# Ten weight-sum steps moved beside attention, two gate tiles made during the loading of attention's result, and one operand sum moved from GpSimd to VectorE

## The chip, the cores and the metric

The kernel runs on one core of a Trainium2 chip. The core has a matrix engine (TensorE, PE in the profile), a vector engine (VectorE, DVE), an activation engine (ScalarE, ACT), a general engine (GpSimd, POOL) and an engine that mostly issues transfers (SyncE, SP). Each engine works through its own instruction queue in order; semaphores tie the queues together. GpSimd issues transfers too, from the same queue as its arithmetic. The metric is the device time of one execution in microseconds (us), lower is better.

## What is computed

One layer of a streaming encoder on 1024 prompt rows and 32 sample rows, 1056 in all, with D = 1024:

```python
h = rms_norm(x, g_mix)
z = h @ w_in
q, k, v, ch, cb, cc, ga, gb = jnp.split(z, SPLITS, axis=-1)
a = attn_core(q, k, v) @ w_attn_out
u = cc * ch
up = jnp.concatenate([conv_left, u], axis=1)
conv = up[:, 0:n] * conv_w[0]
for j in range(1, CONV_WIDTH):
    conv = conv + up[:, j:j + n] * conv_w[j]
bo = (cb * conv) @ w_conv_out
x = x + (jax.nn.sigmoid(ga) * a + jax.nn.sigmoid(gb) * bo) @ w_mix_out
...
x = x + co @ w_co
hm = rms_norm(x, g_mlp)
x = x + jnp.square(jax.nn.relu(hm @ w_up)) @ w_down
```

The attention is a sliding window of 64-frame chunks with 16 query heads and 4 key heads; between the two parts shown stands a cross-attention into 256 memory tokens.

## The kernel before

Activations lie with features on the 128 partitions. The 1056 rows are three chunks, c = 0, 1, 2, of 384, 384 and 288 columns; D is eight feature tiles, f = 0..7. Every fp32 product is made from two rounded halves of each operand, so a weight tile of 128 x 1024 passes through `issue_w`: a load into `wr` (two buffers), a cast into `wh` on ScalarE (L125) and a subtraction into `wl` on VectorE (L126), three buffers each. A product of one weight tile with one chunk (`gemm`, L183 to L185) is 24 matmuls. Weights are fetched in the order in which items are put on a plan (`item`, `worder`), three ahead.

**Weight sums.** Two products later in the kernel, the gate pairs and the down projection, combine blocks of the weights in a scheme that saves multiplications, and need sums of blocks. GpSimd makes these sums early, one piece at a time, in `sum_step` (L691 to L713): a step starts the load of the next piece (L700 or L702) and then does the four additions (L707) and the store (L711 or L713) of the piece before. Its instructions are pinned to their place in program order. There are 46 pieces, 14 for the gates (`gsum_d`) and 32 for down (`wsum_d`), in two buffers that alternate: `xacc`, and `ws` from the pool `W`. A step's load waits until the store from the same buffer, two pieces earlier, has finished. Where no piece is left, a step does nothing.

**Attention.** 32 hosts, i = 0..31, are items that each carry one attention unit inside a projection: scores before the first chunk, `turn` (transposes) after chunk 1, `values` after chunk 2. A host is a convolution tile (C, H or B), a query tile, a key tile, or, the last one, the gate tile f = 0 (`do_gate`). In C hosts GpSimd multiplies by R (L612), in B hosts too (L627); GpSimd also writes the sink column of each unit's scores (L549). A sum step stands after chunk 1 of hosts 3, 5, ..., 31: 15 steps. The results go to `ao_d` in memory, the last two from GpSimd's queue (L594).

**Behind attention.** `load_attended` (L758 to L763) reads `ao_d` back: per chunk eight tiles, each loaded into a `ct` buffer (six of them), cast on ScalarE and subtracted on VectorE. Around these loads stand a second gate tile (w_in 42) and the eight tiles of attn_out. Attn_out's tile f = 0 is multiplied by the gate that the last host made (`sa`) and stored to `m1_d`; the others are stored unmultiplied to `a_d` by a ScalarE copy (L800). After the items of attn_out stand 24 sum steps and, beside them, `gx_steps`, which make operand combinations for the gate pairs, one of them on GpSimd (n4, L839). Then the seven gate pairs, f = 1..7 (`gate_pair`), each with two weight tiles of w_in and two of sums, make both gates of a tile for chunks 0 and 1 by the scheme and for chunk 2 directly (`gate_c2`); they load attn_out's tile back from `a_d`, multiply and store to `m1_d`. They hold three sum steps each.

**Then** `after_gates` closes the pools of X and of the sums (`W`) and opens `mpool` in their place, for the merged tiles M. `do_conv_out` makes for each chunk and f a product, multiplies it by the gate (L1014), adds the stored attention part (L1015, on GpSimd except for f = 7) and splits the result into M; `do_mix` follows. Accumulators in PSUM are three.

Of the kernel before, what the change touches and what calls it, by code (L numbers as in the profile page):

```python
# [10 lines left out]
F32 = mybir.dt.float32  # L11
F32R = mybir.dt.float32r
AF = mybir.ActivationFunctionType
ALU = mybir.AluOpType
# [4 lines left out]
P = 128  # L19
# [3 lines left out]
CH = [(0, 384), (384, 384), (768, 288)]  # L23
# [15 lines left out]
def hybrid_step(ctx: ExitStack, tc: tile.TileContext, io):  # L39
    nc = tc.nc  # L40
    act, dve, pool_e, pe, sp = nc.scalar, nc.vector, nc.gpsimd, nc.tensor, nc.sync
# [3 lines left out]
    def nm(s):  # L45
        uid[0] += 1
        return f"{s}_{uid[0]}"

    def opened(name, **kw):
        cm = tc.tile_pool(name=name, **kw)  # L50
        return cm, cm.__enter__()
# [10 lines left out]
    ps_cm, ps = opened("ps", bufs=1, space=PSUM)  # L62
# [30 lines left out]
    def pin(ins):  # L93
        return tc.keep_in_program_order(ins)

    def acc_tile(shape):
        return ps.tile(shape, F32, tag="acc", bufs=n_acc, name=nm("acc"))
# [3 lines left out]
    def tmp(n, dt=F32):  # L101
        return tp.tile([P, n], dt, tag="ct", bufs=NCT, name=nm("ct"))

    def slot(pool, tag, n, dt=F32R, bufs=None):
        return pool.tile([P, n], dt, tag=tag, bufs=bufs, name=nm(tag))
# [8 lines left out]
    def item(fn, *keys):  # L114
        plan.append((fn, keys))
        worder.extend(keys)
# [61 lines left out]
    def gemm(out, w, acts):  # L178

        wh, wl = w  # L180
        for k, (hi, lo) in enumerate(acts):
            a = slice(k * P, k * P + P)
            pe.matmul(out, wh[:, a], hi, start=(k == 0), stop=False)  # L183
            pe.matmul(out, wh[:, a], lo, start=False, stop=False)  # L184
            pe.matmul(out, wl[:, a], hi, start=False, stop=(k == len(acts) - 1))  # L185
# [13 lines left out]
    R, RC = [None] * 3, [None] * 3  # L199
# [75 lines left out]
    xg = [[None] * NF for _ in CH]  # L275
# [175 lines left out]
    def after(extras, c):  # L451
        for at, e in extras:
            if at == c:
                e()
# [186 lines left out]
    G = {}  # L641

    def gate_slot(c, f):
        n = CH[c][1]
        return slot(ga_pool, f"Ga{c}", n, F32) if f < 3 else slot(G["pool"], f"Gb{c}", n, F32)
# [1 line left out]
    sg = [[None] * NF for _ in CH]  # L647


    sa = [None] * 3  # L650

    def do_gate(to, extras=()):
        def fn(w):
            for c, (o, n) in enumerate(CH):
                a = acc_tile([P, n])
                gemm(a, w, xg[c])
                t = gate_slot(c, 0)
                dve.tensor_mul(t, a, R[c])
                act.activation(t, t, AF.Sigmoid)
                to(c, t)  # L660
                after(extras, c)

        return fn
# [59 lines left out]
    for i, h in enumerate(hosts):  # L723
        kv, p = i // 8, i % 8
        units = [Unit(kv, p)] + ([Unit(kv, 8)] if p == 7 else [])
        pre = []
        if p == 0:
            pre.append(lambda kv=kv: do_KS(kv))
        pre.append(units[0].scores)
        extras = [(1, units[0].turn), (2, units[0].values)]  # L730
        if i == 0:
            extras = [(0, pre.pop()), (2, units[0].turn)]
            first = units[0].values
        if i == 1:
            extras.insert(0, (0, first))
        if p == 7:
            extras += [(0, units[1].scores), (2, units[1].turn), (2, units[1].values)]
        if i % 2 and i > 1:
            extras.append((1, sum_step))
        if h[0] == "Q":  # L740
            fn, key = do_Q(h[1], h[2], extras), qt(h[1], h[2])
        elif h[0] == "K":
            fn, key = do_K(h[1], extras), ("w_in", 8 + h[1])
        elif h[0] == "G":
            fn, key = do_gate(sa.__setitem__, extras), ("w_in", 34)
        else:
            fn, key = do_conv(*h, extras), conv_w(h[1], h[0])
        item(lambda w, fn=fn, pre=pre: ([e() for e in pre], fn(w)), key)
# [41 lines left out]
    def do_attn_out(f, extras=()):  # L790
        def fn(w):
            for c, (o, n) in enumerate(CH):
                a = acc_tile([P, n])
                gemm(a, w, aop[c])
                t = tmp(n)
                if f == 0:
                    dve.tensor_mul(t, a, sa[c])
                    sp.dma_start(m1_d[c][:, f], t)
                else:
                    act.copy(t, a)  # L800
                    sp.dma_start(a_d[c][:, f], t)
                after(extras, c)

        return fn
# [5 lines left out]
    gop, xq = {}, {}  # L810
# [12 lines left out]
    def gx_split(kind, k, c):  # L823
        hi, lo = gop[kind, k] = (slot(xpool, f"X{c}", 384), slot(xpool, f"X{c}", 384))
        pin(act.copy(hi, xq[kind]))
        pin(dve.tensor_sub(lo, xq[kind], hi.bitcast(F32)))
# [9 lines left out]
        gx_split("b21", k, 0)  # L836

    def gx_rest(k):
        pool_e.tensor_tensor(xq["n4"], xq["b21"], xq["t2"], op=ALU.subtract)  # L839
        sp.dma_start(xs_d["n4"][:, k], xq["n4"])  # L840
        gx_split("t2", k, 1)
        gx_split("n1", k, 1)
# [22 lines left out]
    def close_gates():  # L865
# [6 lines left out]
            wanted.extend((bcp[c], k, bc_d[c][:, k], CH[c][1], lambda c=c: yslot(c)) for k in range(NF))  # L872
        pump(2)

    def gate_pair(f):
        def take(key):
            k, w = ready.pop(0)
            assert k == key, (k, key)  # L880
            return w

        def gate_c2(w):
            n = CH[2][1]
            a = ps.tile([P, n], F32, tag="pt", bufs=2, name=nm("pa"))
            gemm(a, w, xg[2])
            return a

        def into(t, x):
            act.activation(t, x, AF.Sigmoid)  # L890
            return t

        def attended(c, t):
            dve.tensor_mul(t, t, la[c])
            sp.dma_start(m1_d[c][:, f], t)

        la = {}

        def load_a(c):
            la[c] = tmp(CH[c][1])  # L900
            sp.dma_start(la[c], a_d[c][:, f])

        op = lambda kind: [gop[kind, k] for k in range(4)]
        w1 = take(("w_in", 34 + f))
        load_a(0)
        load_a(2)
        A, B, C = (acc_tile([P, 384]) for _ in range(3))
        product(A, w1, 0, op("b11"), True)
        s1 = Y["top"].tile([P, 384], F32, tag="s1", name=nm("s1"))
        act.copy(s1, A)  # L910
        issue_w()
        fetch_w()
        product(A, w1, 1, op("b21"), False)
        attended(0, into(tmp(384), A))
        pump(4 if f == 1 else 1)
        a2 = gate_c2(w1)
        t = tmp(CH[2][1])
        dve.tensor_mul(t, a2, R[2])
        attended(2, into(t, t))
        issue_w()  # L920
        fetch_w()
        w4 = take(("g_sum", f - 1, 0))
        product(B, w4, 0, op("t2"), True)
        load_a(1)
        u2 = Y["top"].tile([P, 384], F32, tag="u2", name=nm("u2"))
        dve.tensor_sub(u2, B, s1)
        sum_step()
        pump(4 if f == 1 else 1)
        w3 = take(("g_sum", f - 1, 1))
        product(C, w3, 1, op("n1"), True)  # L930
        v = Y["top"].tile([P, 384], F32, tag="v", name=nm("v"))
        dve.tensor_add(v, C, s1)
        product(B, w3, 0, op("n3"), False)
        g22 = gate_slot(1, f)
        dve.tensor_sub(g22, B, v)
        sg[1][f] = into(g22, g22)
        pump(0)
        sum_step()
        product(C, w4, 1, op("b22"), False)
        t = tmp(384)  # L940
        dve.tensor_sub(t, C, u2)
        attended(1, into(t, t))
        issue_w()
        fetch_w()
        w2 = take(("w_in", 42 + f))
        product(B, w2, 1, op("n4"), False)
        g21 = gate_slot(0, f)
        dve.tensor_sub(g21, B, s1)
        sg[0][f] = into(g21, g21)
        sum_step()  # L950
        issue_w()
        fetch_w()
        a2 = gate_c2(w2)
        g2 = gate_slot(2, f)
        dve.tensor_mul(g2, a2, R[2])
        sg[2][f] = into(g2, g2)
# [4 lines left out]
    item(lambda: [e() for e in ao(0, range(NF))])  # L961
    b0 = [(0, e) for e in ao(1, range(4))] + [(1, e) for e in ao(1, range(4, NF))] + [(2, e) for e in ao(2, range(4))]
    item(do_gate(hold, b0 + [(2, sum_step)]), ("w_in", 42))
    for f in range(NF):
        extras = [(c, sum_step) for c in range(3)]
        if f == 0:
            extras += [(0, e) for e in ao(2, range(4, NF))]
        else:
            extras += [(c, gx_steps.pop(0)) for c in range(3) if gx_steps]
        item(do_attn_out(f, extras), ("w_attn_out", f))  # L970
# [336 lines left out]
    b11, b21, b22 = (lambda k: xm[0][k]), (lambda k: xm[0][k + 4]), (lambda k: xm[1][k + 4])  # L1307
# [517 lines left out]
```

## Time and profile before

| | |
|---|---|
| median of three runs | 1856.05 us |
| lowest and highest | 1848.42 and 1859.84 us |
| time of the profiled execution | 1858.32 us |
| its span, first to last instruction | 1856.5 us |
| mean granted clock of TensorE | 0.978 |
| bytes moved, mean rate over the span | 330.81 MB, 178 GB/s |

The span is 1.8 us shorter than the profiled execution's own time. Times of single instructions, waits and stages come from that one execution. In rows of the timeline the first number is the start after the span's beginning and the second the duration, in us; brackets give the idle time of the engine just before, and what ended it. "x3" counts instructions. Matmul durations overlap, so that work on TensorE is better read from starts, or from the weight loads (PEld).

### The profile page before, as it was taken

Reading aid. Unit: us, or ns where it says so; the run is one execution under the profiler, and the core shown is the slowest. Engines: PE = TensorE matmul, PEld = TensorE weight load, DVE = VectorE, ACT = ScalarE, POOL = GpSimd, SP = SyncE. Lnnn points to the kernel's source line nnn. Section 1 sums busy time; section 2 is a strip of 40 time slices with the busy share of each in tenths; the row PEclk is TensorE's granted clock in tenths of the full one; section 3 lists DMA queues with packets and bytes.
Section 4 is the critical chain, followed back from the end, with each engine's and each line's share of the span. In section 5 each row is a group of like instructions: output and inputs, shape, how many; then the busy total and the mean of one; then the engine's idle time right before and its main releaser. Section 6 shows DMA issues by size and latency. Waiting matters only on the chain. (4 is left out here: it accounts for less than half of the span.)

```text
span 1856.5 us, 30253 instructions
## 1 busy us (share of the span) xinstructions
PE 1759.0 (95%) x11110; PEld 1737.1 (94%) x11110; DVE 1164.0 (63%) x2158; ACT 795.7 (43%) x1566; POOL 600.5 (32%) x685
## 2 busy tenths in 40 slices
PE   8999999999998999962999989999999989999998
PEld 8999999999998999962999989999999979999997
DVE  6776767667656555533657677776665676435673
ACT  8644535344353333312555655642222333324453
POOL 0013242523424545454224242276555400100001
PEclk9999999999999999985999989999999999999999
DMA  4322232323338888756765657663434488446673
GB/s 174 116 90 97 87 126 81 114 77 111 106 119 283 280 280 276 267 212 206 251 225 182 230 198 256 233 224 119 137 132 141 129 260 261 149 135 196 202 232 130
DMA packets 184291, 330.81 MB, mean 178 GB/s; under 512 B 18817, under 2 KB 140193, under 8 KB 184017
## 3 DMA queue, kind: packets, MB, share of 16 engines
q1 hardware_dynamic: 170368, 280.49, 45.9%
q0 software_dynamic: 13776, 48.41, 7.3%
q8 instruction: 87, 1.43, 0.3%
q14 instruction: 60, 0.48, 0.1%
HBM read 241.86 MB, written 86.97 MB: 177 GB/s over the span
## 5 line engine op out<-in xcount | busy, mean ns | idle before, releaser
L126 DVE TENSOR_TENSOR wl<-wr,wh 128x1024 fp32r<-128x1024 f32 x222 | 294.7, 1328 | 203.7 <-ACT wh L125 203.0
L125 ACT CAST wh<-wr 128x1024 fp32r<-128x1024 f32 x222 | 233.0, 1050 | 440.4 <-PE acc L184 103.6
L183 PE MATMUL acc<-X,wh 128*128 128x384 f32 (+1 forms) x864 | 282.3, 327 | 8.3 <-ACT wh L125 8.3
L184 PE MATMUL acc<-X,wh 128*128 128x384 f32 (+1 forms) x864 | 279.6, 324 | 0.0
L185 PE MATMUL acc<-X,wl 128*128 128x384 f32 (+1 forms) x864 | 278.9, 323 | 0.2 <-DVE wl L126 0.2
L183 PE MATMUL acc<-Y,wh 128*128 128x384 f32 (+1 forms) x624 | 203.5, 327 | 56.6 <-DVE ct L1014 51.9
L184 PE MATMUL acc<-Y,wh 128*128 128x384 f32 (+1 forms) x624 | 203.1, 326 | 1.2 <-DVE Y L763 1.0
L185 PE MATMUL acc<-Y,wl 128*128 128x384 f32 (+1 forms) x624 | 202.8, 325 | 0.0
L259 POOL TENSOR_TENSOR xacc<-xacc,ct 128x384 f32<-128x384 f32 (+1 forms) x62 | 75.6, 1221 | 343.8 <-ACT ct L257 342.0
L183 PEld LDWEIGHTS acc<-Y,wh 128*128 128x128 f32 x624 | 117.8, 189 | 59.3 <-ACT Y L781 52.2
L183 PEld LDWEIGHTS acc<-X,wh 128*128 128x128 f32 x864 | 163.2, 189 | 8.9 <-ACT wh L125 8.3
L184 PEld LDWEIGHTS acc<-X,wh 128*128 128x128 f32 x864 | 163.5, 189 | 0.6
L185 PEld LDWEIGHTS acc<-X,wl 128*128 128x128 f32 x864 | 163.2, 189 | 0.8 <-DVE wl L126 0.8
L184 PEld LDWEIGHTS acc<-Y,wh 128*128 128x128 f32 x624 | 118.0, 189 | 2.7 <-DVE Y L763 2.5
L185 PEld LDWEIGHTS acc<-Y,wl 128*128 128x128 f32 x624 | 118.1, 189 | 0.0
L1571 PE MATMUL acc<-Y,wh 128*128 128x384 f32 (+1 forms) x352 | 113.2, 322 | 0.9 <-DVE lt L1362 0.7
L1572 PE MATMUL acc<-Y,wh 128*128 128x384 f32 (+1 forms) x352 | 113.2, 322 | 0.0
L1573 PE MATMUL acc<-Y,wl 128*128 128x384 f32 (+1 forms) x352 | 112.9, 321 | 0.0
L125 ACT CAST PTh<-pt 128x512 fp32r<-128x512 f32 (+3 forms) x94 | 46.2, 516 | 119.3 <-PE pt L572 111.1
L707 POOL TENSOR_TENSOR xacc<-xacc 128x256 f32<-128x256 f32 x92 | 85.6, 930 | 5.4
L851 PE MATMUL acc<-Y,wh 128*128 128x384 f32 x248 | 83.5, 337 | 2.4 <-DVE ct L1224 1.4
L707 POOL TENSOR_TENSOR ws<-ws 128x256 f32<-128x256 f32 x92 | 82.4, 896 | 5.7
(357 smaller groups left out, 4726.0 us busy)
## 6 DMA issues: line engine op xcount, KB each, us to landing
wr<-in_w_in SPq DMA_DIRECT2D x50, 512.0 KB, 3.5
wr<-in_w_up SPq DMA_DIRECT2D x48, 512.0 KB, 3.8
wr<-in_w_down SPq DMA_DIRECT2D x32, 512.0 KB, 3.8
wr<-wsum_d SPq DMA_DIRECT2D x32, 512.0 KB, 3.7
wl<-wl_d SPq DMA_DIRECT2D x28, 512.0 KB, 4.6
wr<-in_w_conv_out SPq DMA_DIRECT2D x24, 512.0 KB, 4.7
wr<-in_w_mix SPq DMA_DIRECT2D x24, 512.0 KB, 5.1
ct<-b_d SPq DMA_DIRECT2D x48, 192.0 KB, 3.8
```

The lines of the kernel that those rows point to most:

```text
L125: act.copy(hi, src)
L126: dve.tensor_sub(lo, src, hi.bitcast(F32))
L183: pe.matmul(out, wh[:, a], hi, start=(k == 0), stop=False)
L184: pe.matmul(out, wh[:, a], lo, start=False, stop=False)
L185: pe.matmul(out, wl[:, a], hi, start=False, stop=(k == len(acts) - 1))
L259: pool_e.tensor_tensor(acc, acc, sq, op=ALU.add)
L707: pin(pool_e.tensor_tensor(t[:, to], t[:, x], t[:, y], op=ALU.add))
L851: pe.matmul(acc, wh[:, a], hi, start=(start and k == 0), stop=False, skip_group_check=True)
L1571: pe.matmul(a, wh[:, s], hi, start=(start and k == 0), stop=False, skip_group_check=True)
L1572: pe.matmul(a, wh[:, s], lo, start=False, stop=False, skip_group_check=True)
L1573: pe.matmul(a, wl[:, s], hi, start=False, stop=(stop and k == len(acts) - 1), skip_group_check=True)
```

## The change

It has three parts.

1. Hosts 12 to 31 all carry a sum step after chunk 1, where before only the odd ones did. That makes 25 steps in attention instead of 15. The steps behind are left as they were; since the pieces are the same 46, the later ones find none left.
2. Chunk 2 of the first gate, for tiles f = 2 and 3, is made by two new items directly behind the second gate tile, while `ao_d` is read back (`gate_a2`). Their weight tiles, w_in 36 and 37, are fetched for it and fetched again for the gate pairs. The two gates stay in `Gb2` buffers until attn_out's tiles 2 and 3 multiply by them on VectorE (instead of the ScalarE copy) and store to `m1_d`; gate pairs 2 and 3 then neither load chunk 2 of `a_d` nor make that gate.
3. The operand n4 is subtracted on VectorE, pinned, instead of on GpSimd (four times).

`sa` becomes a dictionary with the key (chunk, tile), and `gate_c2` moves out of `gate_pair`.

```diff
-        if i % 2 and i > 1:
+        if i % 2 and i > 1 or i > 11:
             extras.append((1, sum_step))
...
-                if f == 0:
-                    dve.tensor_mul(t, a, sa[c])
+                if (c, f) in sa:
+                    dve.tensor_mul(t, a, sa[c, f])
                     sp.dma_start(m1_d[c][:, f], t)
                 else:
                     act.copy(t, a)
...
     def gx_rest(k):
-        pool_e.tensor_tensor(xq["n4"], xq["b21"], xq["t2"], op=ALU.subtract)
+        pin(dve.tensor_sub(xq["n4"], xq["b21"], xq["t2"]))
...
+    def gate_c2(w):
+        n = CH[2][1]
+        a = ps.tile([P, n], F32, tag="pt", bufs=2, name=nm("pa"))
+        gemm(a, w, xg[2])
+        return a
+
+    def gate_a2(f):
+        def fn(w):
+            a = gate_c2(w)
+            t = sa[2, f] = slot(G["pool"], "Gb2", CH[2][1], F32)
+            dve.tensor_mul(t, a, R[2])
+            act.activation(t, t, AF.Sigmoid)
+
+        return fn
...
         def load_a(c):
+            if (c, f) in sa:
+                return
             la[c] = tmp(CH[c][1])
             sp.dma_start(la[c], a_d[c][:, f])
...
-        a2 = gate_c2(w1)
-        t = tmp(CH[2][1])
-        dve.tensor_mul(t, a2, R[2])
-        attended(2, into(t, t))
+        if (2, f) not in sa:
+            a2 = gate_c2(w1)
+            t = tmp(CH[2][1])
+            dve.tensor_mul(t, a2, R[2])
+            attended(2, into(t, t))
...
     item(do_gate(hold, b0 + [(2, sum_step)]), ("w_in", 42))
+    for f in (2, 3):
+        item(gate_a2(f), ("w_in", 34 + f))
     for f in range(NF):
```

More of the change, by code (lines that the diff above doesn't have):

```diff
@@ L647, in hybrid_step @@
     sg = [[None] * NF for _ in CH]
-    sa = [None] * 3
+    sa = {}
     def do_gate(to, extras=()):
@@ L744, in hybrid_step @@
         elif h[0] == "G":
-            fn, key = do_gate(sa.__setitem__, extras), ("w_in", 34)
+            fn, key = do_gate(lambda c, t: sa.__setitem__((c, 0), t), extras), ("w_in", 34)
         else:
@@ L881, in take @@
             return w
[L883 to L887, printed above, removed]
         def into(t, x):
```

## The prediction

> **What bounds the kernel now.** I read the page's first two parts, then busy time by stage, then the timeline of the one stage where TensorE stops.
>
> ```profile
> span 1856.5 us, 30253 instructions
> PE 1759.0 (95%) x11110; PEld 1737.1 (94%) x11110; DVE 1164.0 (63%) x2158; ACT 795.7 (43%) x1566; POOL 600.5 (32%) x685
> ...
> PE   8999999999998999962999989999999989999998
> ...
> POOL 0013242523424545454224242276555400100001
> PEclk9999999999999999985999989999999999999999
> ```
>
> TensorE is the bound: 95% of the span, full in almost every slice of 46.4 us. The one deep hole is at slices 18 and 19 (6 and 2), and there the granted clock falls too (8 and 5). GpSimd is busy in just those slices. So a saving anywhere else must shorten TensorE's own work, and a saving in the hole can be large. The stages around it (columns: length, busy time and count of each engine, granted clock, DMA share, GB/s):
>
> ```profile
> core 0: us, PE busy (x) PEld busy (x) DVE busy (x) ACT busy (x) POOL busy (x), PEclk, DMA share, GB/s
> ...
> 86.00:556.00 470.00, 470.00 (x3043) 463.36 (x3042) 323.84 (x825) 208.71 (x503) 157.89 (x244) 1.00 0.31 103
> 556.00:582.00 26.00, 20.77 (x111) 17.66 (x110) 16.94 (x27) 10.94 (x23) 13.14 (x19) 1.00 0.84 278
> 582.00:803.60 221.60, 221.60 (x1391) 221.60 (x1390) 125.75 (x168) 79.26 (x140) 107.16 (x130) 1.00 0.82 274
> 803.60:820.40 16.80, 16.80 (x98) 16.68 (x96) 7.07 (x7) 3.88 (x5) 7.91 (x9) 1.00 0.72 252
> 820.40:872.40 52.00, 0.20 (x2) 0.00 (x0) 7.12 (x10) 5.25 (x10) 25.42 (x36) 0.53 0.56 194
> 872.40:940.00 67.60, 66.28 (x364) 65.36 (x365) 44.14 (x66) 32.72 (x56) 17.57 (x15) 0.96 0.70 234
> ```
>
> In order these are attention (32 hosts, 14.7 us each), attention's result loading under attn_out's first tile, attn_out and the gate pairs, the first four conv_out tiles, a stop of 52.0 us, and the rest of conv_out and mix for chunk 0. What ends the stop, in the timeline:
>
> ```profile
> 820.26 0.34 PE L185 MATMUL acc<-Y,wl 128*128 128x384 f32 x1
> ...
> 858.82 0.55 POOL L702 DMA_DIRECT2D ws<-in_w_down  x1 [4.40 <-DMA wsum_d<-ws]
> ...
> 867.20 0.57 POOL L713 DMA_DIRECT2D wsum_d<-ws  x1 [0.41 <-POOL ws L707]
> 870.29 0.51 ACT L125 CAST M<-ct 128x384 fp32r<-128x384 f32 x1 [6.64 <-DMA wsum_d<-ws]
> ...
> 871.78 0.55 DVE L1014 TENSOR_TENSOR ct<-acc,Ga 128x384 f32<-128x384 f32 x1
> ...
> 872.48 0.66 PE L183 MATMUL acc<-Y,wh 128*128 128x384 f32 x1 [51.88 <-DVE ct L1014]
> ```
>
> Read from the bottom up: TensorE waits for a free accumulator, that is for VectorE's eviction L1014; it stands behind the split of the first merged tile M; M waits for the store of the last weight sum. M's pool lies where the sums' buffer `ws` was (`after_gates`). GpSimd still makes weight sums 47 us after TensorE stopped. The stop is a late finish of the sums and nothing else that I can see.
>
> **Part 1, ten more sum steps in attention.** How late are the sums? Each is a load, four additions and a store on GpSimd's queue:
>
> ```profile
> 552.30 0.68 POOL L702 DMA_DIRECT2D ws<-in_w_down  x1
> ...
> 758.72 0.54 POOL L702 DMA_DIRECT2D ws<-in_w_down  x1 [4.64 <-DMA wsum_d<-ws]
> ```
>
> ```profile
> L707 POOL TENSOR_TENSOR ws<-ws 128x256 f32<-128x256 f32 x64 | 57.4, 896 | 4.1
> ...
> L713 POOL DMA_DIRECT2D wsum_d<-ws x16 | 9.2, 574 | 6.1 <-POOL ws L707 6.1
> ...
> L702 POOL DMA_DIRECT2D ws<-in_w_down x15 | 8.0, 536 | 66.8 <-DMA wsum_d<-ws 66.8
> L839 POOL TENSOR_TENSOR Gb<-Gb,Gb 128x384 f32<-128x384 f32 x4 | 4.8, 1202 | 9.5 <-DVE X L826 9.5
> ```
>
> The load at 552.30 is piece 16 of 46; piece 36 starts at 758.72, so a piece takes (758.7 - 552.3)/20 = 10.3 us, of which 4 x 0.90 + 0.57 + 0.54 = 4.7 is work and the rest waiting for the buffer's store. The last load is at 858.82 and its store lands by 870.3. With 25 instead of 15 steps inside attention, piece 26 starts near 552; the last of the 20 that remain is loaded where piece 36 stands now, near 759, and its store lands 11.5 us later, about 770. The first M is wanted when the first conv_out tile is done, 803.6 + 4.2 = 808. The sums then have 38 us to spare, so the stop goes whole: **-52.0 us**. With it goes the cold restart:
>
> ```profile
> 872.40:876.00 3.60, 3.52 (x11) 3.56 (x12) 3.44 (x7) 1.74 (x4) 1.05 (x1) 0.50 0.56 165
> 876.00:880.00 4.00, 4.00 (x19) 4.00 (x18) 1.76 (x4) 1.83 (x5) 1.00 (x1) 0.73 0.65 210
> 880.00:884.00 4.00, 4.00 (x25) 4.00 (x24) 4.00 (x7) 2.12 (x4) 1.15 (x1) 1.00 0.54 159
> ```
>
> At 0.50 for 3.6 us and 0.73 for 4.0 us, 1.8 + 1.1 = **-2.9 us**.
>
> What is late next at that place? During the stop the queues went on filling buffers: 52.0 us x 194 GB/s = 10.1 MB, of which five loads and six stores of sums, 11 x 0.52 = 5.8 MB, so 4.3 MB for conv_out were fetched for nothing. They must now travel beside TensorE. From 803.6 to 940 without the stop that makes 4.2 MB less some 1.6 MB of sums, plus 4.3, plus 67.6 x 234 = 15.8 MB: 22.7 MB in 84.4 us, 269 GB/s. Between 582.0 and 803.6 the chip held 274 GB/s with TensorE never idle, so it just fits. Bounds: 0, and 4.3 MB at 274 GB/s = 15.7 us if nothing can be overlapped. I take **+3 us**, near the lower end, because that full stage is the nearest row.
>
> Inside attention the ten pieces add 10 x 4.7 = 47 us to GpSimd's 157.9 of 470. GpSimd's queue is in order, and the steps stand ahead of the multiplications by R that the convolution waits for, of the sink column of the next scores, and of two stores of attention's result. The nearest rows are stretches where sums already came densely:
>
> ```profile
> 360.00:380.00 20.00, 20.00 (x127) 19.79 (x126) 13.24 (x39) 6.88 (x20) 13.15 (x21) 1.00 0.53 180
> 420.00:440.00 20.00, 20.00 (x132) 19.68 (x132) 18.05 (x53) 11.20 (x32) 2.91 (x5) 1.00 0.30 101
> ```
>
> With GpSimd 13.15 of 20 us busy, the weight loads (19.79) are no less dense than in the stretch with 2.91 (19.68). A host has 14.7 us, and a step of 4.7 beside three multiplications of 1.2 (L839's row has that shape) fits. The exposed case is the second row, VectorE at 18.05 of 20 with few sums beside it; such a stretch now gets some. Bounds: 0 and 16 us (rival C). I take **+1**. The two result stores on GpSimd's queue may move by one piece, 10.3 us; the tiles they feed are the last ones loaded in a stage of 26 us, so nothing.
>
> **Part 2, two chunk-2 gate tiles in the load phase.** The work that moves, first matmul of such a tile and the first behind it:
>
> ```profile
> 784.65 0.29 PE L183 MATMUL pa<-X,wh 128*128 128x288 f32 x1
> ...
> 787.85 0.34 PE L851 MATMUL acc<-X,wh 128*128 128x384 f32 x1
> ```
>
> 24 matmuls take 3.2 us, two tiles 6.4. They leave a stage where TensorE is full (221.60 of 221.60) and go to one where weight loads fill 17.66 of 26.0 us, 8.3 us open. The hole there is made by the loads of attention's result:
>
> ```profile
> L762 ACT CAST Y<-ct 128x384 fp32r<-128x384 f32 (+1 forms) x20 | 8.8, 478 | 11.5 <-DMA ct<-ao_d 11.5
> ...
> wr<-in_w_in SPq DMA_DIRECT2D x50, 512.0 KB, 3.5
> ```
>
> Gain: at most 6.4 us. Cost: the two weight tiles are fetched twice, 1.05 MB more, in a stage that moves 278 GB/s at a DMA share of 0.84: 3.8 us later results if none of it overlaps. Two of the reloads stand on SyncE's queue among the result's last loads; VectorE gets two more weight splits and ahead of later splits of the result waits for the two gate tiles. The end is therefore between 6.4 gained and, if the extra fetch delays all and fills nothing, 3.8 lost. The two matmul blocks themselves need nothing that is late (X has lain there since the start), so they do run in the hole: I take **-4 us**. Each of the two gate pairs also loses one load of 147 KB and a multiplication, neither on TensorE's path.
>
> **Part 3, n4 to VectorE.** Four additions leave GpSimd, 4.8 us and 9.5 us of waiting that stood among the sums: the sums end up to 14 us sooner, where they already have 38 to spare. VectorE gets four operations of 384 columns (its 1024 column splits take 1.2 us, row under rival C) in a stage where it is busy 125.75 of 221.60. Nothing either way; it is a reserve for part 1.
>
> **Sum.** The profiled execution took 1858.3 us (span 1856.5), 2.3 above the median of the three runs. 1858.3 - 52.0 - 2.9 + 3 + 1 - 4 = 1803.4, and 2.3 less on the median's scale: 1801. I say **1802**.
>
> **Rivals.** A: a new shortage takes part of the place of the stop. Either conv_out becomes bound by transfers (15.7 instead of 3: 1815) or half of the ten steps are not absorbed, the sums end near 770 + 5 x 10.3 = 822, and 14 us of stop remain (1816). For: 269 against 274 GB/s is tight. Against: the four first conv_out tiles ran without a gap at 252 GB/s. Chance 0.12.
>
> B: slower than before. GpSimd becomes the bound of attention: if a step costs not 4.7 but its 10.3 us (the store's wait in line) and each of the three multiplications 3.6 (L839's 4.8 and 9.5 over four), a host with such multiplications takes 21.1 instead of 14.7 us, and ten of the last 20 hosts have them (the conv items C and B): 1802 + 64 = 1866. It decides from 55/10 = 5.5 us a host. Against: in attention steps are a host apart and a buffer has been stored long before; where sums already crowd, TensorE is full. Chance 0.03.
>
> C: VectorE is slowed by GpSimd. The weight split's rows spread:
>
> ```profile
> L126 DVE TENSOR_TENSOR wl<-wr,wh x39: 1207/1225/1753, 557.8 to 816.1; 128x1024 fp32r<-128x1024 f32 x39
> ```
>
> Median 1.225, longest 1.753, 43% more. If all additional additions in attention (10 x 4 x 0.9 = 36 us) slowed VectorE so, it would need 16 us more, and if all of it showed on TensorE the time is 1802 - 1 + 16 = 1817. VectorE is idle for 146 us of attention, so most should vanish. Chance 0.06. The Trainium skill has this as a rule (GPSIMD Engine Reference, section Specifications): GpSimd shares its SBUF interfaces with VectorE, and contends with VectorE instructions that take two SBUF inputs; the split is such an instruction, and the spread agrees.
>
> D: the change does not do what it says: something else than the sums holds M's space, and the stop stays. Then only part 2 and the costs are left, 1856 - 4 + 1 = 1853. Against: the releaser of M is the sum's store by name, and the last other reader of that pool, the last gate pair, ends at 803.6. Chance 0.04.
>
> **Numbers.** Forecast 0.75, A 0.12, C 0.06, D 0.04, B 0.03. The forecast's own range: part 2 at its full 6.4, no cost at conv_out and attention gives 1795, and the runs of before lie from 8 below to 4 above their median; with part 2 at nothing and a few microseconds more of costs 1811. To hold A and C as well the range is 1792 to 1818; D and B are left out. One per cent, 18.6 us, is about what a measurement of this kernel can tell from no change. Faster by more than that: forecast, A and C, 0.93; within: D, 0.04; slower: B, 0.03.
>
> **What would show it.** Right: the last `wsum_d` store near 770 or earlier, no gap of tens of microseconds at conv_out's first tiles, a granted clock of 1.00 through that stage, attention still 470 us long, the load phase with some 6 us more of weight loads in it and gate pairs of f = 2 and 3 3.2 us shorter. Wrong: M's first split released by another store or load; TensorE waiting for wr in conv_out (A); hosts from the 13th on longer than 14.7 us with TensorE released by GpSimd's Ga or ct (B) or by VectorE (C).

## The result, and the profile after

| | before | changed |
|---|---|---|
| median | 1856.40 us (4 runs) | 1805.28 us (4 runs) |
| lowest and highest | 1848.42 and 1859.84 us | 1803.02 and 1808.78 us |
| profiled execution, and its span | 1858.32, 1856.5 us | 1804.14, 1802.0 us |

The ratio of the changed kernel to the one before is 0.9732, with a 95% interval of 0.9697 to 0.9768: faster by 51 us. On the scale of the profiled executions the prediction's sum was 1803.4 us; 1804.14 was measured.

The first parts of the page of the changed kernel, span and busy time first, then the slices of 45 us:

```profile
span 1802.0 us, 30258 instructions
PE 1756.7 (97%) x11110; PEld 1736.2 (96%) x11110; DVE 1172.4 (65%) x2164; ACT 797.2 (44%) x1566; POOL 593.8 (33%) x681
...
PE   8999999999999999999999999999999899999998
...
POOL 0013245653454444502224242385555300100101
PEclk9999999999999999999999989999999999999999
```

The hole is gone from TensorE's row and from the clock's. TensorE's busy time is almost what it was (1756.7 against 1759.0), so the 54.5 us of span are idle time removed. GpSimd's sums, which stood in slices 18 and 19, now stand in slices 7 to 12, where four of its six digits have grown.

The stages of the changed kernel, cut at nearly the same places as before (length, busy time and count of TensorE, weight loads, VectorE, ScalarE and GpSimd, granted clock, DMA share, GB/s):

```profile
86.00:555.90 469.90, 469.90 (x3040) 463.09 (x3039) 334.08 (x825) 208.51 (x502) 203.41 (x304) 1.00 0.37 125
555.90:582.00 26.10, 23.59 (x137) 22.35 (x136) 18.37 (x30) 12.68 (x26) 11.56 (x16) 0.93 0.86 297
582.00:800.00 218.00, 216.50 (x1347) 215.29 (x1346) 124.94 (x167) 77.32 (x134) 89.02 (x112) 1.00 0.77 263
800.00:817.00 17.00, 17.00 (x101) 17.00 (x100) 10.08 (x16) 7.78 (x13) 2.87 (x2) 1.00 0.83 287
817.00:885.00 68.00, 65.66 (x374) 64.24 (x372) 46.82 (x71) 35.85 (x61) 15.48 (x14) 1.00 0.79 267
```

Attention has GpSimd busy for 203.41 us instead of 157.89 and is no longer for it: TensorE is busy in all of it. Behind 817 us, where the stop was, TensorE is busy for 65.66 of 68.00 us at a clock of 1.00. Two things are less good than the rest: the loading stage has a clock of 0.93, and the gate pairs, which were full before, now have 1.5 us of TensorE's idle time.

What happens to the sums and to M, in the timeline (start, duration, idle time before and what ended it):

```profile
757.05 0.55 POOL L702 DMA_DIRECT2D ws<-in_w_down  x1 [5.00 <-DMA wsum_d<-ws]
...
767.63 0.57 POOL L713 DMA_DIRECT2D wsum_d<-ws  x1 [0.41 <-POOL ws L707]
807.88 1.00 POOL L1031 TENSOR_TENSOR ct<-ct,ct 128x384 f32<-128x384 f32 x1 [39.68 <-DMA mkr<-mk_d]
...
810.71 0.51 ACT L125 CAST M<-ct 128x384 fp32r<-128x384 f32 x1
```

The last load stands at 757.05 and the last store at 767.63; then GpSimd has nothing to do for 39.68 us, until conv_out's first tile wants its addition. (The row names a load as the releaser; the addition's own operand, the eviction L1030, is ready at 807.74.) ScalarE has no idle time any more before M's first split.

How long conv_out's eight tiles of chunk 0 take, from the first matmul of conv_out to the first of mix, before and then in the changed kernel (its first row, 555.56, is the first matmul behind attention and its second gate tile; this is called the end of attention below, and stands at 555.80 in the kernel before):

```profile
803.66 0.34 PE L183 MATMUL acc<-Y,wh 128*128 128x384 f32 x1
...
891.91 0.33 PE L183 MATMUL acc<-M,wh 128*128 128x384 f32 x1
```

```profile
555.56 0.30 PE L183 MATMUL pa<-X,wh 128*128 128x288 f32 x1
...
802.79 0.34 PE L183 MATMUL acc<-Y,wh 128*128 128x384 f32 x1
...
836.32 0.33 PE L183 MATMUL acc<-M,wh 128*128 128x384 f32 x1
```

88.25 us became 33.53 us, 54.7 less. Eight tiles at the pace of the first four, which ran without a gap before (4.19 us each), are 33.5: conv_out now runs at full rate. The span is 54.5 us shorter, so this one place is the whole change. Conv_out starts 0.9 us earlier than before, and what follows mix's first matmul takes 965.7 instead of 964.6 us.

### The profile page after: what moved, and what is told of

It reads as the page before. It is cut to its first block, busy times and chain, and to the rows that moved or that the text cites. A ratio compares the mean times of both kernels' runs of the same rounds, so it can differ in the third digit from the quotient of the medians.

```text
span 1802.0 us, 30258 instructions
## 1 busy us (share of the span) xinstructions
PE 1756.7 (97%) x11110; PEld 1736.2 (96%) x11110; DVE 1172.4 (65%) x2164; ACT 797.2 (44%) x1566; POOL 593.8 (33%) x681
## 5 line engine op out<-in xcount | busy, mean ns | idle before, releaser
L126 DVE TENSOR_TENSOR wl<-wr,wh 128x1024 fp32r<-128x1024 f32 x224 | 298.0, 1330 | 169.8 <-ACT wh L125 158.4
L1588 PE MATMUL acc<-Y,wh 128*128 128x384 f32 (+1 forms) x352 | 113.6, 323 | 0.0
L1244 POOL TENSOR_TENSOR ct<-ct 128x288 f32<-128x288 f32 (+1 forms) x48 | 45.1, 941 | 119.0 <-DVE ct L1240 45.6
```

The costliest lines, as they stand in the source:

```text
L126: dve.tensor_sub(lo, src, hi.bitcast(F32))
L1244: pool_e.tensor_tensor(h, t, t, op=ALU.mult)
L1588: pe.matmul(a, wh[:, s], lo, start=False, stop=False, skip_group_check=True)
```

## The experiments

The runs came in three groups, each with its own runs of the kernel before (median 1856.37, 1850.93 and 1858.06 us), so times of different groups are compared by their ratios.

### The first part alone

The kernel before with the first part of the change and nothing else:

```diff
-        if i % 2 and i > 1:
+        if i % 2 and i > 1 or i > 11:
```

> The kernel before with part 1 alone: 25 sum steps in attention, gate tiles and n4 as before. If the late sums are the whole gain, the stop of 52.0 us and its cold restart go: about 1856 - 54 = 1802 plus what parts 2 and 3 are worth, which the landmarks of the two profiles put at 0.6 us, so 1800 to 1808, and no gap over 3 us at the first conv_out tiles. If the three parts are needed together (the reserve from part 3, the shorter gate pairs from part 2), some 10 to 20 us of stop remain: 1815 to 1825.

Measured: 1802.71 us (1800.79 to 1804.89), ratio 0.9713 (0.9692 to 0.9734). The last store of a sum was issued at 771.47 us and conv_out started at 803.77. As far as times can tell, the first part is the whole gain.

### The change without the second part

The two items go, so `sa` holds only the tiles of f = 0:

```diff
-    for f in (2, 3):
-        item(gate_a2(f), ("w_in", 34 + f))
```

> The changed kernel without part 2 (no gate tiles behind attention, gate pairs 2 and 3 as before). If part 2 is worth the 4 us that I summed, this is about 1809. If it gives back in the gate pairs what it gains in the load phase (landmarks: 3.1 us ahead behind attn_out's second tile, 0.9 us ahead at conv_out), this is within 2 us of the changed kernel, 1804 to 1808, and the gaps of 2 us in all at 682 to 687 us of the changed kernel's trace are not there.

Measured: 1804.5 us (1799.84 to 1807.2), ratio 0.972 (0.9698 to 0.9743). The second part is worth nothing that the time can tell. The last store was issued at 754.79 us, 16.7 us sooner than in the kernel with the first part alone, which lacks the third; attention ended 2.1 us sooner in this execution, so the third part gives some 14.6 us of GpSimd's queue. A second profile of the first part alone (below) has its last store 3.4 us sooner behind the end of attention, which leaves 11.2. That is what the prediction said (up to 14) and, as it said, nobody needs it while the sums are early. The third part without the first wasn't run: there those 11 to 15 us would come off the stop, if it follows the sums as in the next experiment.

### Three steps more instead of ten

```diff
-        if i % 2 and i > 1:
+        if i % 2 and i > 1 or i > 25:
```

> The kernel before with three more sum steps in attention (hosts 26, 28 and 30) in place of ten. If each step moved is worth one piece of GpSimd's chain, the last store lands 3 x 10.3 = 31 us sooner, the first split of M starts near 870.3 - 31 = 839, the stop is about 21 us instead of 52.0, and the time about 1825. If what matters is only that the sums end before the gate pairs, or that something else holds M's space, the stop stays near 52 and the time near 1856.

Measured: 1828.04 us in one run. The chain that ends the stop, in the timeline of this kernel:

```profile
830.97 0.57 POOL L713 DMA_DIRECT2D wsum_d<-ws  x1 [0.41 <-POOL ws L707]
834.02 0.51 ACT L125 CAST M<-ct 128x384 fp32r<-128x384 f32 x1 [18.48 <-DMA wsum_d<-ws]
836.20 0.66 PE L183 MATMUL acc<-Y,wh 128*128 128x384 f32 x1 [15.17 <-DVE ct L1014]
```

The same three instructions in the same order as in the kernel before, 36 us earlier, and a stop of 15.2 instead of 51.9 us. Three steps took 36.7 us off and the last store moved by the same 36.2, which is 12 us a step and more than the 10.3 expected. The stop thus follows the sums. Conv_out's eight tiles took 55.66 us, only 32.6 less than before, because TensorE waited once more for an eviction (2.33 us at 853.93) and restarted at half clock (0.50 from 836 to 840 us). The rows also give the rule: TensorE comes back 5.2 us behind the last store's issue, as in the kernel before (5.3), and it stops only where conv_out's fourth tile ends (820.4 in the kernel before), not where M is first wanted (808), since three accumulators let it run on. TensorE's return lies 2.2 us behind M's first split (834.02 to 836.20), so by that the sums may end some 10 us later than the prediction allowed.

### The second part alone

The kernel before with the two early gate tiles and with 15 steps as before:

> The kernel before with part 2 alone. The stop stays, since it ends when the sums end, whatever TensorE did before: whichever worth part 2 has in the gate pairs, the first split of M stays near 870 us and the time near 1856, at most 1 us off for this; the stop grows by as much as conv_out starts sooner. If part 2 frees the sums in some way (its fewer loads in the gate pairs), the time falls by 3 us or more.

Its edit is the part of the change that makes, keeps and uses `sa[2, f]`, as shown in the change. Measured: 1862.38 us in one run. Conv_out started 2.8 us earlier than before, and then:

```profile
868.23 0.57 POOL L713 DMA_DIRECT2D wsum_d<-ws  x1 [0.41 <-POOL ws L707]
872.18 0.51 ACT L125 CAST M<-ct 128x384 fp32r<-128x384 f32 x1
874.36 0.66 PE L183 MATMUL acc<-Y,wh 128*128 128x384 f32 x1 [56.55 <-DVE ct L1030]
```

The stop grew to 56.55 us. While the sums are late, whatever TensorE saves ahead of them is waited for again, and the sums ended 1 us later still, for which the extra loads are a likely cause that wasn't tested. The time was expected within 1 us of 1856; this one run is 4 us above the slowest of the seven runs of the kernel before, so part of it isn't explained.

### Other tiles made early

The changed kernel gains little from the second part. Its timeline shows two places, the loading stage and the gate pair f = 2 (TensorE, with the idle time before and who ended it):

```profile
570.46 0.44 PE L183 MATMUL acc<-Y,wh 128*128 128x384 f32 x1 [0.56 <-ACT Y L762]
...
573.83 0.93 PE L183 MATMUL acc<-Y,wh 128*128 128x288 f32 x2 [1.62 <-ACT Y L762]
...
682.39 0.44 PE L853 MATMUL acc<-X,wl 128*128 128x384 f32 x1 [0.32 <-DVE wl L126]
686.50 0.44 PE L851 MATMUL acc<-X,wh 128*128 128x384 f32 x1 [1.00 <-ACT wh L125]
687.29 0.44 PE L851 MATMUL acc<-X,wh 128*128 128x384 f32 x1 [0.18 <-ACT s L923]
```

TensorE still waits for attention's result, and in pair 2 it now waits twice for weight halves and once for the copy `s`, as it didn't before. The next run makes other tiles early:

```diff
-    for f in (2, 3):
+    for f in (5, 6):
```

> The changed kernel, but the two chunk-2 gate tiles made early are f = 5 and 6 instead of 2 and 3. Theory: the loading stage still gains about 3 us from them, and the 2.0 to 2.3 us that the changed kernel lost at 682 to 687 us (TensorE waiting for weight halves) came because pair 2, where the operand splits and n4 still run on VectorE and ScalarE, had lost the chunk-2 block that covered them. Pairs 5 and 6 have no such neighbours, so the stalls go, conv_out starts at 800 to 801.5 us instead of 802.8, and the time is 1803, not to be told from 1805. Rival: any pair that loses its chunk-2 block stalls for its weight split, so the same 2 to 4.5 us are lost in pairs 5 and 6 (730 to 785 us) and conv_out starts at 802.5 to 805.

Measured: 1798.48 us (1796.05 to 1802.58), ratio 0.9723 (0.9699 to 0.9747). The three waits of pair 2 are gone and pairs 5 and 6 have none. The end of attention and the start of conv_out:

```profile
554.06 0.30 PE L183 MATMUL pa<-X,wh 128*128 128x288 f32 x1
...
797.67 0.34 PE L183 MATMUL acc<-Y,wh 128*128 128x384 f32 x1
```

From the end of attention to conv_out it takes 243.6 us, against 247.2 in the changed kernel (246.5 in its second profile): 3.6 us less, somewhat more than expected. In the time itself this can't be told; the ratio lies inside the other's interval.

### A third tile

```diff
-    for f in (2, 3):
+    for f in (4, 5, 6):
```

> The changed kernel with three chunk-2 gate tiles made early, f = 4, 5 and 6. TensorE's loading stage has 2.5 us open behind two tiles. Theory (each tile is 3.2 us of work, but its weights are another 0.5 MB in a stage whose transfers are at their limit): the third tile gains 0 to 1.5 us, the end of attn_out's tile f = 1 moves from 590.0 to 592 to 593.5 us, and conv_out starts at 799 to 802. Rival (the hole is there for the taking): a full 3.2 us more, conv_out at 797 to 799. Other rival (the extra load delays attention's result): the end of tile f = 1 moves by 3.5 us or more and conv_out starts later than in the run with tiles 5 and 6.

Measured: 1801.92 us in one run; conv_out started at 797.3 us, 240.7 behind the end of attention. The rival that took the hole as there for the taking was right. The kernel was timed in the next group, beside the changed kernel, the first part alone, and the three tiles together with 29 steps in attention:

> The changed kernel itself once more, as the yardstick on the chip of the next three runs. Theory (part 1 is the whole gain, part 2 as it was made is worth 0.6 us): equal to the kernel with part 1 alone within 0.3%, 0.971 to 0.974 of the kernel before; conv_out starts 247 us after the end of attention. Rival (parts 2 and 3 are worth something that one profile hid): 3 us or more below the kernel with part 1 alone.

> The kernel before with part 1 alone, on the same chip as the changed kernel. Theory: within 3 us of it, conv_out starts 247.8 us after the end of attention as in the kernel before. Rival: 3 to 5 us above it.

> The changed kernel with tiles 4, 5 and 6 made early, timed. Its first profile had conv_out start 240.7 us after the end of attention, 6.5 us less than the changed kernel, with no gap left in the gate pairs. Theory: the same again, and a time 4 to 7 us below the changed kernel's. Rival (the single profile was a lucky one; the third tile's weights delay attention's result in other executions): within 2 us of the changed kernel.

> Tiles 4, 5 and 6 early, and 29 steps in attention. Theory (the sums were early enough, so more steps in attention are worth nothing but the freed transfers of the loading stage): conv_out starts 239 to 241 us after the end of attention, time 0 to 2 us below that of the run with tiles 4, 5 and 6 alone. Rival (denser sums slow VectorE in attention, seen in the run with doubled steps as 2.9 us of TensorE waiting): attention 0.5 to 2 us longer, time 0 to 2 us above.

| kernel | median, us | ratio to before | attention's end to gate pairs | gate pairs | sum, to conv_out |
|---|---|---|---|---|---|
| before (its first profile) | 1858.06 | 1 | 100.3 | 147.6 | 247.9 |
| changed | 1804.59 | 0.9708 (0.9683 to 0.9732) | 103.8 | 142.7 | 246.5 |
| first part alone | 1802.06 | 0.9697 (0.9672 to 0.9723) | 99.5 | 147.8 | 247.4 |
| tiles 4, 5, 6 | 1802.95 | 0.9703 (0.968 to 0.9726) | 103.2 | 137.8 | 241.0 |
| tiles 4, 5, 6 and 29 steps | 1805.24 | 0.9707 (0.9682 to 0.9733) | 103.4 | 137.8 | 241.1 |

The last three columns are differences between first matmuls in each timeline (behind attention, of the gate pairs, of conv_out). The theory of the first two runs held, the ratio 0.9708 at its edge. For the third the path to conv_out is 5.5 us shorter again, yet the time, which the theory put 4 to 7 us below, is the same: its number is the rival's, its path is not. The fourth run's path is that of the third; its attention ended 1.2 us later (556.28 against 555.10 us) and its time was 2.3 us above, which would suit its rival, but the intervals lie on each other. Where the lead goes is seen 660 us later, at the opening of the down projection. First the kernel with tiles 5 and 6, VectorE and then TensorE; the fold additions (L1444) combine down's operands, L782 splits the hidden layer for the matmul L1588, the last row:

```profile
1456.04 0.55 DVE L1577 TENSOR_TENSOR Ga<-acc,Ga 128x384 f32<-128x384 f32 x1
...
1457.90 2.02 DVE L782 TENSOR_TENSOR H<-ct,H 128x288 fp32r<-128x288 f32 x5
1461.83 0.56 DVE L1444 TENSOR_TENSOR fold<-fold,fold 128x384 f32<-128x384 f32 x1 [1.92 <-DMA fold<-b_d]
...
1458.40 0.40 PE L1588 MATMUL acc<-H,wh 128*128 128x288 f32 x1 [2.78 <-DVE H L782]
```

Then the kernel with tiles 4, 5 and 6 (the timed one):

```profile
1461.17 0.56 DVE L1444 TENSOR_TENSOR fold<-fold,fold 128x384 f32<-128x384 f32 x1 [5.19 <-DMA fold<-b_d]
1461.65 0.55 DVE L1577 TENSOR_TENSOR Ga<-acc,Ga 128x384 f32<-128x384 f32 x1
...
1463.51 0.45 DVE L782 TENSOR_TENSOR H<-ct,H 128x288 fp32r<-128x288 f32 x1
...
1464.01 0.61 PE L1588 MATMUL acc<-H,wh 128*128 128x288 f32 x1 [9.03 <-DVE H L782]
```

VectorE's order is another one here. With tiles 5 and 6 the evictions L1577 and H's splits stand ahead of the fold addition that waits for a load; with tiles 4, 5 and 6 that addition stands first, VectorE waits 5.19 us for its load, and everything behind it, TensorE's H included, waits too: 9.03 instead of 2.78 us. All profiles with three tiles show this gap (9.0 to 10.1 us), those with two or none 2.3 to 3.5. The additions and evictions on that stretch aren't pinned, and their order came out differently; that this order is the cause is read from the traces. Pinning it as it was is the open step, and it wasn't tried. So no kernel that was run beats the changed one by what a measurement can tell.

### Four steps more

The changed kernel with a step in each host from host 3 on, 29 in attention:

```diff
-        if i % 2 and i > 1 or i > 11:
+        if i > 2:
```

> The changed kernel with a sum step in every host from the third on, 29 instead of 25 in attention. Theory: the sums end about 41 us sooner (four pieces of 10.3 us), near 720 us; they were early enough already, so the stop stays at zero, attention stays 470 us, and the time is 1803 to 1806. Rival (dense sums hurt VectorE or TensorE's hosts in the first half of attention, where VectorE has 18 of 20 us of work): attention grows by 1 to 6 us and the time is 1806 to 1812. Other rival (four fewer pieces to load and store beside the transfers of the loading stage and the pairs free the memory queues): the small gaps at 566 to 578 us shrink and the time is 1800 to 1803.

Measured: 1805.35 us (1796.14 to 1807.34), ratio 0.9764 (0.974 to 0.9789). The last store was issued at 726.03 us, 41.6 us sooner than in the changed kernel (36.3 sooner than in its second profile; 41 were expected), and it is worth nothing. The loading stage was 1.8 us shorter than in the changed kernel (101.9 instead of 103.7 us), in favour of the last rival. But the time doesn't show it, and the other pair of kernels with and without these four steps (103.4 and 103.2 us in the table) doesn't repeat it.

### A second step in each of the later hosts

From host 12 on, each host gets a second step:

```diff
+            if i > 11:
+                extras.append((2, sum_step))
```

> The changed kernel with a second sum step behind chunk 2 of each host from the thirteenth on, so that nearly all 46 pieces are made in attention and two stand in each of the later hosts. It asks where rival B of the prediction begins. GpSimd alone needs at least 7.4 us for a piece (822.13 to 829.55 in the kernel before, without other work), two make 14.8, and a convolution host adds three multiplications of 1.2 us: 18.4 us against a host of 14.7. If GpSimd bounds such hosts, those ten of the last twenty become 3 to 4 us longer: attention 500 to 507 us, TensorE released by GpSimd's multiplications, time about 1835 to 1845. If the store's wait overlaps with the multiplications or the hosts between give the time back, attention stays within 3 us of 470 and the time is 1803 to 1808. The pieces end inside attention or just behind it either way.

Measured: 1809.7 us in one run; attention ended at 558.05 us instead of 555.56, 2.5 later, with the hosts not 3 to 4 us longer. But the run doesn't show two steps in a host. At the end of attention the loads of 36 of the 46 pieces had been started, against 26 in the changed kernel: ten of the twenty added steps slid behind attention, and the last store was issued at 669.63 us. From 266.83 to 557.41 us the loads of 31 pieces were started, one each 9.7 us, where two in a host of 14.7 would need 7.3. The pinned instructions keep their order among themselves only. The hosts' multiplications stand in GpSimd's queue between the additions of one piece (in the changed kernel too), and the two result stores L594, which stand behind all 45 steps in the program, ran at 559.48 and 563.23 us, ahead of the 37th load. What TensorE waited for, in the timeline of this kernel, was not GpSimd:

```profile
325.13 0.30 PE L584 MATMUL o<-PTh,VS 128*128 128x128 f32 x1 [1.11 <-DVE AO L591]
327.13 0.53 PE L572 MATMUL pt<-ident,S 128*128 128x128 f32 x2 [0.71 <-DVE S L564]
```

VectorE was late. Its groups between 260 and 556 us (busy time and mean ns of one behind the bar), in the kernels before, changed, and with doubled steps:

```profile
L126 DVE TENSOR_TENSOR wl<-wr,wh 128x1024 fp32r<-128x1024 f32 x20 | 27.7, 1386 | 8.0 <-ACT wh L125 8.0
L564 DVE TENSOR_SCALAR S<-S,rec 128x256 f32<-128x256 f32 (+1 forms) x83 | 25.9, 372 | 0.7
L625 DVE SCALAR_TENSOR_TENSOR ct<-u,prm,ct 128x384 f32<-128x384 f32 (+1 forms) x30 | 18.8, 632 | 2.3 <-ACT ct L623 2.1
```

```profile
L564 DVE TENSOR_SCALAR S<-S,rec 128x256 f32<-128x256 f32 (+1 forms) x83 | 30.7, 430 | 0.7
L126 DVE TENSOR_TENSOR wl<-wr,wh 128x1024 fp32r<-128x1024 f32 x20 | 27.7, 1387 | 7.9 <-ACT wh L125 7.9
L625 DVE SCALAR_TENSOR_TENSOR ct<-u,prm,ct 128x384 f32<-128x384 f32 (+1 forms) x30 | 22.3, 747 | 2.3 <-ACT ct L623 2.1
```

```profile
L564 DVE TENSOR_SCALAR S<-S,rec 128x256 f32<-128x256 f32 (+1 forms) x83 | 35.6, 488 | 0.7
L126 DVE TENSOR_TENSOR wl<-wr,wh 128x1024 fp32r<-128x1024 f32 x20 | 29.1, 1455 | 6.6 <-ACT wh L125 6.6
L625 DVE SCALAR_TENSOR_TENSOR ct<-u,prm,ct 128x384 f32<-128x384 f32 (+1 forms) x30 | 26.1, 875 | 2.4 <-ACT ct L623 2.1
```

The multiplication L564 goes from 372 over 430 to 488 ns, L625 from 632 over 747 to 875. This is rival C at work (the last section sorts single instructions). In the changed kernel it hides in VectorE's idle time; with the further steps it comes through in one stretch of 12 us.

## Why the prediction was right, step by step

**What bounds the kernel.** Shown by experiment: TensorE's hole was the late sums and nothing else. Ten steps remove it, three remove 36.7 us of it, and the second part without them is no gain.

**The stop, -52.0, and the restart, -2.9.** Together -54.9 predicted, -54.7 measured (88.25 to 33.53 us for the eight tiles). The last load was put near 759 and stood at 757.05; the last store was to land about 770, and it was issued at 767.63. The price of 10.3 us a piece behind attention was therefore right. The slack of 38 us is seen as GpSimd's 39.68 us of idle time; it was itself some 10 us too small, since TensorE can run three more tiles ahead.

**Transfers in conv_out, +3 (0 to 15.7).** In conv_out nothing came: 33.53 us for eight tiles is full rate. The part 800 to 885 us moved 267 to 287 GB/s, about the 269 that was computed, with TensorE full in the first 17 us of it. In mix, which the term covers too, something did: TensorE waits 1.55 us at 852.62 for a weight half, whose cast on ScalarE stood behind a wait of 1.51 us for a load of cross-attention (1.89 us in the kernel with the first part alone). The kernel before had waits of 2.5 us in the same stage, so by the cross-attention the account is even, and the lower bound was the value.

**Attention, +1 (0 to 16).** -0.2: its end moved from 555.80 to 555.56 us. The mechanism of the upper bound is real, as L564 and L625 show, but VectorE's busy time rose by 10 us instead of 16, from 323.84 to 334.08, and it had 146 idle.

**The second part, -4 (-6.4 to +3.8).** This term was the worst sized one. Conv_out starts 247.2 us behind attention instead of 247.9: -0.6 (-1.4 in the second profile). The loading stage did take in the work: with 6.4 us more in it, it became 3.4 us longer, a gain of 3.0 that is near the 4 forecast. What failed is the sentence that the two gate pairs lose nothing on TensorE's path. The pairs should have become 6.4 us shorter, 147.6 to 141.2, and became 143.5. The chunk-2 block of pair 2 had covered the weight split of the next product; with the block gone, TensorE waits at 682 to 687 us for `wl` and `wh`. In the shorter wait (0.32 us) VectorE had been splitting N first. The longer one (1.00 us) has another cause, as ScalarE's row shows:

```profile
685.40 1.04 ACT L125 CAST wh<-wr 128x1024 fp32r<-128x1024 f32 x1 [4.60 <-PE acc L852]
```

ScalarE was idle for 4.60 us, and the cast began when a matmul had ended, which fits a wait for one of the three `wh` buffers. Tiles 5 and 6 lose nothing of that kind (pairs of 141.1 us). That a neighbour's work can cover a split is shown by this; why pair 2 is the tender one stays open.

**The third part, nothing.** Shown, with the first part in place, by the two runs with and without it: the sums end 11 to 15 us sooner behind attention, and the time is the same.

**The rivals.** A, a new shortage in conv_out, didn't come, and its price for five unabsorbed steps was too high: by the run with three more steps, sums that end at 822 would have left 822 + 2 - 820.4, some 4 us of stop, not 14 (2 us from the store's landing to TensorE's return, 834.02 to 836.20 there). B didn't come: the row of attention shows TensorE busy for all of 469.90 us. Where it would begin isn't shown, since in the run with doubled steps half of the added steps slid behind attention. That the steps stand ahead of the multiplications, as B and the cost in attention suppose, holds only in part there. C's mechanism is there, hidden. D fell with the first run.

**The number.** The sum of the terms was 1803.4 us on the scale of a profiled execution and 1804.1 came out; the forecast of the median was 1802 (range 1792 to 1818), and 1805.28 was measured. That the -54.9 came true is the mechanism. That the rest fits to a microsecond is luck, because two misses cancel: conv_out's +3 and attention's +1 were not paid, and most of the second part's 4 were not earned. The cross-attention begins 55.8 us earlier than before, and 1.3 us of that is lost again behind it in this execution.

## What to carry to other kernels

Where an engine works ahead for a later stage, find the last instruction that still belongs to it and what its buffers hold back: the time such work may take is counted to where the bounding engine really stops, and past that nearly each microsecond shows as a stop, before it none. A block that is moved off a full engine into a hole can leave a place where it covered something; look for new waits there, and try another block of the same kind. A lead won on the bounding engine can be lost where the unpinned order of another engine changes: compare that order far behind the change, too.

## What the runs showed of the hardware

**The clock falls after short waits too.** In the changed kernel's loading stage the clock was at half from 573.38 to 576.79 us. The windows on both sides of the fall (TensorE's busy time is the first figure behind the length, the granted clock stands third from the end):

```profile
569.97:573.38 3.41, 1.59 (x6) 0.99 (x6) 1.53 (x3) 0.97 (x3) 0.79 (x2) 1.00 1.00 355
573.38:576.79 3.41, 2.96 (x9) 2.96 (x10) 2.98 (x4) 2.00 (x5) 3.05 (x4) 0.50 0.95 320
```

This cost about 1.5 us, half of the 2.96 us in which TensorE worked at that rate. The fall comes within an idle time of 1.62 us. The changed kernel's second profile has the same dip with a wait of 1.70 us, while the kernel with tiles 5 and 6 has a like wait at the same place (1.67 us) and no dip. What decides can be read from the traces: within each of the 14, all changes of the clock lie on one grid of 3.41 us. In the kernel with tiles 5 and 6 a border of its grid divides the wait:

```profile
568.20:571.61 3.41, 2.07 (x9) 1.14 (x8) 1.52 (x3) 1.01 (x2) 0.59 (x2) 1.00 1.03 374
571.61:575.02 3.41, 2.56 (x15) 2.56 (x16) 2.58 (x3) 1.60 (x4) 3.08 (x4) 1.00 0.93 290
```

TensorE was busy for 61% and 75% of these two windows, and for 47% of the one before the fall. Over all 14 traces, 72 of 75 falls stand behind a window with at most 55.6% (the other three, 65 to 73%, at the ends of programs), and of some 7100 windows at full clock without a fall behind them 13 have less than that, none less than 47.5%. So the busy share of a window of this grid decides, near one half, and with it the grid's phase; the length of one wait doesn't. The Trainium skill (TensorE: Matmul & The Clock Gate, section "What's actually happening") puts the fall to half rate behind at least one idle window of about 3.4 us, and the return behind about as long a busy one. The length of the window and the return agree with these rows. The fall doesn't: the window needn't be idle, half of it idle is enough, so waits of 2 us can't be taken as safe by that figure.

**GpSimd slows a VectorE instruction while it computes beside it.** The means above mix two kinds. Sorted, in the traces, by whether an arithmetic instruction of GpSimd ran at the same time (260 to 556 us; mean ns of one, in the kernels before, changed, and with doubled steps):

| | alone | beside GpSimd | number beside GpSimd |
|---|---|---|---|
| L564, 128x256 | 364, 369, 365 | 515, 707, 738 | 9, 17, 22 of 75 |
| L625, 128x384 | 612, 613, 610 | 601, 919, 1100 | 2, 11, 11 of 20 |
| L126, weight split, 128x1024 | 1224, 1223, 1222 | 1494, 1442, 1513 | 12, 15, 16 of 20 |
| L126, from PSUM, 128x512 | 682, 684, 687 | 689, 687, 685 | 24, 28, 25 of 38 |

Alone, an instruction takes the same in all three kernels, though the transfers grew from 101 over 138 to 169 GB/s: it is GpSimd that lengthens them. The weight split suffers too; its mean hardly moved (1386, 1387, 1455 ns) because most splits stood beside GpSimd already before the change. The Trainium skill (GPSIMD Engine Reference, section Specifications) names VectorE instructions in a two-port mode or with two SBUF inputs as those that contend with GpSimd. L625 and the weight split, with two inputs in SBUF, agree, and so does the split from PSUM, which has one and isn't slowed. L564 has one tile and a column of factors as inputs; whether it runs in a two-port mode no run here shows. Nor do the runs settle how much longer an instruction gets: single ones beside GpSimd took from the same time as alone up to 3.3 times that (L564, 1219 ns).
